# First modulation vectors in four column strips of TensorE, tokens loaded first, first dense products by halves of the features

## The chip, the cores and the metric

One NeuronCore of a Trainium2 chip runs the kernel. The metric is device time in microseconds for one execution. TensorE is called PE below, VectorE DVE, ScalarE ACT, GpSimd POOL, and SyncE, which issues nearly all transfers, SP.

## What is computed

Two layers of a backbone for 512 latent tokens (x) and 256 context tokens (c), 1024 features, all in float32. Cut to what matters here:

```python
for l in range(2):
    mx = split(silu(c) @ w_mod[l] + b_mod[l], 6)          # six vectors of 1024: shift, scale, gate, twice
    mc = split(silu(c_ctx) @ w_mod[l] + b_mod[l], 6)
    hc = rmsnorm(ctx, g_pre_mix[l]) * (1 + mc[1]) + mc[0]
    h  = rmsnorm(x,   g_pre_mix[l]) * (1 + mx[1]) + mx[0]
    p  = h @ w_in[l]          # decays, keys, queries, values, gates, convolution and spatial-gating inputs
    y  = mixers(p)            # short conv | bidirectional gated DeltaNet in chunks | spatial gating
    x  = x + mx[2] * rmsnorm(y @ w_o[l], g_post_mix[l])
    ...                       # then a SwiGLU feed-forward, modulated by mx[3], mx[4], mx[5]; the context likewise
```

So nothing dense can start before shift and scale of the first norm are there: columns 0 to 2047 of `w_mod[0]`, 8.4 MB, multiplied by two vectors of 1024.

## The kernel before

Products of float32 operands are made from high and low parts (`hh`, `hl` of the features, `wh`, `wl` of the weights): three one-pass matmuls in a rounded format per 128 rows of contraction. Only the modulation, transposes and a few small sums are plain float32 matmuls.

**Who sets the order.** `Builder` writes the program along an estimated timeline: each part of the work is a task that yields a time or a condition, and of the tasks that can go on the one with the lowest priority number does (`run_tasks`). PE keeps the order written. Tables of numbers (`K`) hold priorities, depths and the events that tasks wait for. Every transfer is issued on SP (`dma`, line 430).

**Opening.** `cond` makes `csilu`, the silu of the two conditioning vectors as 128 x 16. `mod_pe` (line 804) takes `w_mod` in tiles `mw` of 128 rows x 512 columns (256 KB). Eight of them, the contraction, make one block of 512 columns: `ps[:2, :] += csilu[:, k::8]^T mw`, two rows of a bank `ps`. The four blocks come in the order 2, 3 (scale), 0, 1 (shift); 6 tiles may be loaded ahead. `mod_columns` turns the two rows into columns by four small transposes (`modr`), adds the bias, and `mod_ready` derives the factors when both blocks of a part are there. `layer_vectors` loads the biases, gains and convolution taps as rows `vrows` by eight small transfers and transposes them once.

**Norms.** `start` loads a stream's tokens only when half of block 2 (context) or block 3 (x's event is `half0_1`) has been multiplied, then `pre_norm` (line 874) squares, waits for all of shift and scale, scales by the reciprocal root (`xn`), transposes 128 x 128 pieces into a bank and modulates each of 8 feature tiles: `hh` on ACT, `hu` = high part less shift on ACT, low part on DVE.

**First dense products.** `keys` (line 1052) takes the first three weights (16 columns of decays and rates, the keys and the queries of head 0) stream by stream: all of the context's, then all of x's, so that neither waits for the other.

```python
for s, cond in zip(sts, conds or ()):
    yield cond                                   # hc0, then hx0
    for i, job in enumerate(jobs[:staged]):      # staged = 3
        ...
        yield from self.accumulate(ps, ws[i], self.hl(s[1]), (0, s[0].T), width(job))
```

Behind them follow the decays (`gates`, their rows `rh`), the triangular systems, the inverse of the context's chunks (DVE, `ivt`, `ivv`, `ivb`), that of x's, the scans, the output projections (`yh`) and the feed-forward. Modulation blocks 4 and later come mostly elementwise on DVE (`macc`), some on PE. Buffers of up to 512 columns are handed out from 66 slots; smaller ones share a slot if one is half used.

## Time and profile before

| | |
|---|---|
| median of 3 runs | 1831.14 us (1827.82 to 1832.52) |
| span of the profiled execution | 1826.1 us; its page gives no other time of it |
| PE, DVE, ACT busy | 97%, 70%, 41% of the span |
| read from memory | 233 MB, 136 GB/s over the span |

The page is one execution by the hardware profiler, and its span runs from the first to the last instruction. A share of busy time is a mean over stages with different limits, and PE's busy time is modelled. The window view gives the same per stretch, the timeline the instructions one by one, the views of waits who released whom.

### The profile page before, as it was taken

The page shows a single profiled execution, that of the slowest core. Times are in us where ns is not written, and L with a number is a line of the kernel's source. Part 1 is how long each engine was busy: PE and PEld are TensorE (multiplying, and loading weights), DVE is VectorE, ACT ScalarE, POOL GpSimd, SP SyncE. Part 2 cuts the span into 40 slices and gives each one's busy share as a digit, 9 for nine tenths or more (in the row PEclk, how much of TensorE's full clock was granted, in tenths as well). Part 3 has the DMA queues.
Part 4 walks back from the last instruction along what each step waited for, and adds up shares of the span by engine and source line. Part 5 has one row for each costly group of instructions (what it writes and reads, how often), then busy time and mean ns, then how long its engine had stood idle before and what let it go on. Part 6 is the DMA issues. An engine that isn't in the chain of part 4 may idle for free.

```text
span 1826.1 us, 27432 instructions
## 1 busy us (share of the span) xinstructions
PE 1765.4 (97%) x10319; PEld 1495.7 (82%) x10319; DVE 1269.5 (70%) x2414; ACT 750.3 (41%) x1659; POOL 107.1 (6%) x267
## 2 busy tenths in 40 slices
PE   7899999979999999999999999999899999999998
PEld 2588788869799888888788899878789898888886
DVE  1899877958769877623679867679968884344446
ACT  3764446254474222111464435467343752212122
POOL 0011002101000000000002000003000100000000
PEclk9999999989999999999999999999999999999999
DMA  8742321235578755533352436433333763333334
GB/s 281 249 129 83 95 67 36 79 112 164 173 223 273 222 177 188 153 104 116 106 156 81 127 118 174 137 93 86 89 127 116 230 198 93 100 96 93 104 93 138
DMA packets 288869, 250.15 MB, mean 137 GB/s; under 512 B 14544, under 2 KB 219350, under 8 KB 288736
## 3 DMA queue, kind: packets, MB, share of 16 engines
q1 hardware_dynamic: 288736, 248.40, 44.9%
q8 instruction: 81, 1.33, 0.3%
q14 instruction: 52, 0.43, 0.1%
HBM read 233.28 MB, written 15.07 MB: 136 GB/s over the span
## 4 chain that ended last, share of the span: by engine, by line
PE 71%; DVE 14%; ACT 6%; DMA 4%; issue 3%; POOL 2%; SPq 1%; DVEq 0%; POOLq 0%; ACTq 0%
PE ps L453 69%; DVE wl_l L465 2%; DVE ivt_l L465 2%; PE ps L457 2%; ACT junk L509 2%; DVE ivv_l L465 2%; DMA mw_b<-in_w_mod_dram 1%; ACT wh_l L509 1%; DVE dt_b L465 1%; DVE ivb_l L481 1%; DVE iva_l L481 1%; ACT L509 1%; SPq L430 1%; ACT xn_b L509 1%; DVE macc_b L461 1%
## 5 line engine op out<-in xcount | busy, mean ns | idle before, releaser
L453 PE MATMUL ps<-hh_b,wh_l 128*128 128x256 f32 (+2 forms) x2640 | 726.9, 325 | 8.1 <-DVE hh_b L461 2.5
L453 PE MATMUL ps<-hh_b,wl_l 128*128 128x512 f32 (+2 forms) x2000 | 665.2, 333 | 1.5 <-DVE wl_l L465 1.5
L453 PEld LDWEIGHTS ps<-hh_b,wh_l 128*128 128x128 f32 (+1 forms) x2640 | 456.3, 189 | 61.1 <-issue 5.5
L453 PE MATMUL ps<-hl_b,wh_l 128*128 128x512 f32 (+2 forms) x1360 | 483.9, 356 | 0.0
L465 DVE TENSOR_TENSOR wl_l<-wf_l,wh_l 128x1024 fp32r<-128x1024 f32 (+1 forms) x301 | 362.3, 1206 | 151.3 <-ACT wh_l L509 143.4
L453 PEld LDWEIGHTS ps<-hh_b,wl_l 128*128 128x128 f32 (+1 forms) x2000 | 377.0, 188 | 40.0 <-DVE wl_l L465 2.1
L509 ACT ACTIVATE wh_l<-wf_l 128x1024 fp32r<-128x1024 f32 x197 | 205.0, 1042 | 374.4 <-DMA wf_l<-in_w_ffn_in_dram 119.0
L453 PEld LDWEIGHTS ps<-hl_b,wh_l 128*128 128x128 f32 (+1 forms) x1360 | 256.6, 189 | 33.7 <-issue 0.2
L453 PE MATMUL ps<-wh_l,ah_b 128*128 128x512 f32 x576 | 204.6, 390 | 0.0
L453 PE MATMUL ps<-wl_l,ah_b 128*128 128x512 f32 x440 | 171.6, 390 | 0.9 <-DVE wl_l L465 0.8
L473 DVE CAST wh_l<-wf_l 128x1024 fp32r<-128x1024 f32 (+1 forms) x104 | 71.5, 687 | 130.7 <-PE ps L453 47.3
L461 DVE SCALAR_TENSOR_TENSOR macc_b<-mw_b,csilu,macc_b 128x512 f32<-128x512 f32 x196 | 142.5, 747 | 19.7 <-DMA mw_b<-in_w_mod_dram 13.2
L453 PEld LDWEIGHTS ps<-wh_l,ah_b 128*128 128x128 f32 x576 | 108.1, 188 | 22.9 <-DVE ah_b L465 0.3
L453 PE MATMUL ps<-wh_l,al_b 128*128 128x512 f32 x304 | 118.4, 389 | 0.0
L453 PEld LDWEIGHTS ps<-wl_l,ah_b 128*128 128x128 f32 x440 | 82.6, 188 | 18.6 <-DVE wl_l L465 1.8
L509 ACT ACTIVATE at_b<-ps 128x512 f32<-128x512 f32 (+1 forms) x71 | 33.9, 480 | 127.1 <-PE ps L453 122.0
L509 ACT ACTIVATE ah_b<-at_b 128x512 fp32r<-128x512 f32 (+1 forms) x62 | 33.4, 538 | 108.7 <-DVE at_b L465 108.7
L453 PE MATMUL ps<-wh_l,yh_b 128*128 128x512 f32 x192 | 74.1, 404 | 0.1
L453 PEld LDWEIGHTS ps<-wh_l,al_b 128*128 128x128 f32 x304 | 57.1, 188 | 11.8
L465 DVE TENSOR_TENSOR ivt_l<-ivv_l,ivb_l 128x31 f32<-128x31 f32 (+15 forms) x124 | 60.1, 485 | 3.5
L453 PE MATMUL ps<-wl_l,yh_b 128*128 128x512 f32 x160 | 62.6, 391 | 0.0
L465 DVE TENSOR_TENSOR at_b<-ps,at_b 128x512 f32<-128x512 f32 (+1 forms) x71 | 38.8, 547 | 31.8 <-PE ps L453 31.8
(511 smaller groups left out, 2140.8 us busy)
## 6 DMA issues: line engine op xcount, KB each, us to landing
wf_l<-in_w_ffn_in_dram SPq DMA_DIRECT2D x132, 512.0 KB, 4.5
mw_b<-in_w_mod_dram SPq DMA_DIRECT2D x208, 256.0 KB, 4.3
wf_l<-in_w_ffn_out_dram SPq DMA_DIRECT2D x66, 512.0 KB, 3.8
wf_l<-in_w_in_dram SPq DMA_DIRECT2D x64, 512.0 KB, 4.1
wf_l<-in_w_o_dram SPq DMA_DIRECT2D x32, 512.0 KB, 3.7
us_b<-sd SPq DMA_DIRECT2D x26, 256.0 KB, 2.8
xd<-x_b SPq DMA_DIRECT2D x20, 256.0 KB, 4.6
x_b<-xd SPq DMA_DIRECT2D x20, 256.0 KB, 2.9
```

Source lines behind the costliest of these rows:

```text
L430: self.nc.sync.dma_start(out, in_)
L453: self.nc.tensor.matmul(out, lhsT, rhs, start=start, stop=stop)
L457: self.nc.tensor.transpose(out, in_, self.ident[:m, :m])
L461: self.nc.vector.scalar_tensor_tensor(out=out, in0=in0, scalar=scalar, in1=in1, op0=op0, op1=op1)
L465: self.nc.vector.tensor_tensor(out=out, in0=a, in1=b, op=op)
L473: self.nc.vector.tensor_copy(out, in_)
L481: self.nc.vector.transpose(out, in_)
L509: self.nc.scalar.activation(out=out, in_=in_, func=func, **kw)
```

## The change

- `mod_pe` multiplies tile k into strip `32 * (k % 4)` of the bank: 32 columns of the array, with a stationary operand of 32 columns (`cs4`: the two vectors and 30 zeros), so that four consecutive tiles use four strips. A sum over the strips (`sel4`) takes the place of the transposes. 16 tiles may be loaded ahead in place of 6. The blocks come in the order 2, 0, 3, 1, so scale and shift of the first 512 features are complete after two blocks.
- Tokens of both streams and the first two weights are loaded ahead of `w_mod`. The eight small transfers of `vrows` are issued on ACT.
- `pre_norm` with `halves` squares, scales and transposes without waiting, and modulates four features when their half of the factors is there; `mod_ready` derives factors by block.
- `keys` takes the three staged products by halves of the contraction (the context's queries alone stay whole), both streams in each half.
- `cs4` takes half of a slot and is never freed, so buffers of 256 columns use its other half one after another.

```diff
-     'mpe': 6,
+     'mpe': 16,
...
-    def dma(self, out, in_):
-        self.nc.sync.dma_start(out, in_)
+    def dma(self, out, in_, side=False):
+        (self.nc.scalar if side else self.nc.sync).dma_start(out, in_)
...
+        self.sel4 = self.cp.tile([P, 32], F32, name="sel4")
+        self.vtt(self.sel4, self.ident[:, 0:32], self.ident[:, 32:64], ALU.add)
+        for g in (2, 3):
+            self.vtt(self.sel4, self.sel4, self.ident[:, 32 * g:32 * g + 32], ALU.add)
...
-        ld = lambda r0, ap, n: self.dma(rows[r0:r0 + n, :], ap)
+        ld = lambda r0, ap, n: self.dma(rows[r0:r0 + n, :], ap, l == 0)
...
+        self.cs4 = self.blk("cs4", 32 * KD).ap.rearrange("p (k m) -> p k m", k=KD)
+        self.pset(self.cs4, 0.0)
+        self.vcopy(self.cs4[:, :, 0:2], s.rearrange("p (s k) -> p k s", k=KD))
...
-            yield from self.mod_columns(v, b, ps, (0, 1))
+            r = self.blk("modr")
+            self.act(r.ap, ps)
+            pc = yield from self.gtile(r.ap)
+            for i in range(4):
+                self.matmul(pc[:, 2 * i:2 * i + 2], r.ap[:, P * i:P * i + P], self.sel4[:, 0:2])
+            r.free()
+            self.mod_bias(v, b, pc, streams)
...
-            self.matmul(ps[:2, :], self.csilu[:, k::8], raw.ap, start=(k == 0), stop=(k == KD - 1))
+            g = 32 * (k % 4)
+            self.matmul(ps[g:g + 32, :], self.cs4[:, k, :], raw.ap, start=(k < 4), stop=(k >= 4), share=3)
...
-        yield self.modulated(v["l"], part, part + 1)
-        self.ev.add(name)
+        if not halves:
+            yield self.modulated(v["l"], part, part + 1)
+            self.ev.add(name)
...
+            if halves:
+                yield lambda: all(f"block{v['l']}_{2 * p + hf}" in self.ev for p in (part, part + 1))
+                self.ev.add(name if hf else name + "_half")
...
-        for s, cond in zip(sts, conds or ()):
-            yield cond
-            for i, job in enumerate(jobs[:staged]):
-                if len(ws) == i:
-                    ws.append((yield from feed.take()))
-                yield self.room(8)
-                ps = yield from self.bank()
-                yield from self.accumulate(ps, ws[i], self.hl(s[1]), (0, s[0].T), width(job))
...
+        for hf in range(2 if staged else 0):
+            for s, cond in zip(sts, conds[hf]):
+                yield cond
+                st = s[0]
+                for i, job in enumerate(jobs[:staged]):
+                    whole = st.T < SEQ and i == staged - 1
+                    if whole and not hf:
+                        continue
...
+                    yield from self.accumulate(ps, ws[i], self.hl(s[1]), (0, st.T), width(job),
+                                               range(KD) if whole else range(4 * hf, 4 * hf + 4))
...
-            yield on("half0_2" if st is sc else K["wx"])
             xs = self.load(st, src)
-            yield from self.pre_norm(st, xs, vs[0], 0, hs, name=name)
+            yield from self.pre_norm(st, xs, vs[0], 0, hs, name=name, halves=True)
...
-        spawn(0, self.mod_pe(0, vs[0], [2, 3, 0, 1], (0, 1), K["mpe"]))
-        spawn(0, start(sc, I["ctx"][0], cx, hc, "hc0"))
-        spawn(0, first_weights())
-        spawn(K["plv"], self.layer_vectors(0, vs[0]))
-        spawn(K["psx"], start(sx, I["x"][0], x, hx, "hx0"))
+        spawn(-1, self.layer_vectors(0, vs[0]))
+        spawn(0, start(sc, I["ctx"][0], hc, "hc0"))
+        spawn(0, start(sx, I["x"][0], hx, "hx0"))
+        spawn(0, self.mod_pe(0, vs[0], [2, 0, 3, 1], (0, 1), K["mpe"]))
+        f.add(self.keys_w(0, False) + self.cols_w(0, OFF_V, NH))
```

Line 453 of the kernel before (the matmul of the helper) is line 452 of the changed one. The order in which the program issues its work moves at three places that matter below.

**PE, first products of the modulation.** Before (`mw` are tiles of `w_mod`, `modr` the two rows of a finished block):

```order
L457 MATMUL ps_65<-ident,vrows_b_8_130 128x128
L453 MATMUL ps_64<-mw_b_9_141,csilu 2x512
L453 MATMUL ps_64<-mw_b_10_144,csilu 2x512
L453 MATMUL ps_66<-mw_b_11_147,csilu 2x512
L453 MATMUL ps_66<-mw_b_12_150,csilu 2x512
```

With the change (`cs_b_2_116` is the slot that `cs4` shares, first with `vrows`; `xn` are scaled tokens):

```order
L457 MATMUL ps_64<-ident,cs_b_2_116 128x128
L452 MATMUL ps_65<-mw_b_17_164,cs_b_2_116 32x512
...
L452 MATMUL ps_65<-mw_b_23_176,cs_b_2_116 32x512
L457 MATMUL ps_64<-ident,xn_b_63_257 128x128
L452 MATMUL ps_65<-mw_b_24_178,cs_b_2_116 32x512
L457 MATMUL ps_64<-ident,xn_b_64_259 128x128
L457 MATMUL ps_64<-ident,xn_b_65_261 128x128
L457 MATMUL ps_64<-ident,xn_b_66_263 128x128
L452 MATMUL ps_67<-sel_106,modr_b_75_289 128x2 x4
```

The first seven products stand behind the transpose of `vrows`, the eighth and all later ones behind the first transpose of x's scaled tokens (`xn_b_63`).

**ACT, ahead of those scaled tokens.** With the change:

```order
L509 ACTIVATE pick_122<-ones 128x1 x2
L428 DMA cs_b_2_116<-in_b_mod_dram 48x128
...
L428 DMA cs_b_2_116<-in_g_onorm_dram 1x128
L509 ACTIVATE xn_b_45_225<-x_b_5_138,rx_c 128x512
L509 ACTIVATE junk,sx_x<-x_b_9_147 128x512
...
L509 ACTIVATE junk,sx_x<-x_b_16_159 128x512
L509 ACTIVATE xn_b_63_257<-x_b_9_147,rx_x 128x512
```

Eight transfers are issued here and eight squares of x follow; before, ACT issued none, and x's squares stood behind block 1's rows.

**PE, end of the modulation.** With the change (`hh_b_40`, the context's fourth feature):

```order
L452 MATMUL ps_63<-hh_b_40_220,wh_l_35_205 128x256 x2
L452 MATMUL ps_63<-hh_b_40_220,wl_l_36_206 128x256
L452 MATMUL ps_69<-mw_b_81_314,cs_b_2_116 32x512
L452 MATMUL ps_69<-mw_b_82_317,cs_b_2_116 32x512
L452 MATMUL ps_69<-mw_b_83_320,cs_b_2_116 32x512
L452 MATMUL ps_65<-sel_106,modr_b_95_404 128x2 x4
L457 MATMUL ps_68<-ident,xn_b_85_352 128x128
```

The last three of the 32 products stand behind the dense products of the first four features of the context; before, all 32 stood ahead of every dense product.

## Rows read from the trace of the kernel before

**Rows 1.** The page, busy time of each engine.

```profile
PE 1765.4 (97%) x10319; PEld 1495.7 (82%) x10319; DVE 1269.5 (70%) x2414; ACT 750.3 (41%) x1659; POOL 107.1 (6%) x267
```

**Rows 2.** Windows of the opening: busy us per engine (instructions), granted clock, DMA share, GB/s.

```profile
25.00:30.00 5.00, 5.00 (x13) 1.02 (x12) 0.00 (x0) 1.52 (x3) 0.00 (x0) 1.00 1.05 388
...
40.00:45.00 5.00, 2.57 (x18) 1.41 (x16) 1.64 (x7) 5.00 (x16) 0.00 (x0) 1.00 0.67 213
...
45.00:50.00 5.00, 1.24 (x7) 0.69 (x7) 1.16 (x4) 4.04 (x10) 1.02 (x1) 0.72 0.71 221
...
50.00:55.00 5.00, 4.92 (x27) 4.56 (x28) 4.94 (x11) 5.00 (x11) 0.00 (x0) 0.60 1.05 349
```

**Rows 3.** Timeline of the opening: start us, us, engine, line, operation, tiles.

```profile
4.43 7.87 PE L453 MATMUL ps<-mw_b,csilu 128*2 128x512 f32 x12 [1.25 <-DMA mw_b<-in_w_mod_dram]
...
7.43 0.33 SPq L430 DMA_DIRECT2D vrows_b<-in_b_mod_dram  x1
...
12.21 0.22 SPq L430 DMA_DIRECT2D vrows_b<-in_g_onorm_dram  x1
...
19.56 0.63 ACT L509 ACTIVATE junk<-x_b 128x512 f32<-128x512 f32 x1
...
20.31 0.63 ACT L509 ACTIVATE junk<-x_b 128x512 f32<-128x512 f32 x1
...
20.86 17.33 PE L453 MATMUL ps<-mw_b,csilu 128*2 128x512 f32 x40 [1.18 <-DMA mw_b<-in_w_mod_dram]
...
38.22 0.59 ACT L509 ACTIVATE modr_b<-ps 2x512 f32<-2x512 f32 x1 [6.28 <-DMA x_b<-in_x_dram]
...
40.04 0.24 DVE L469 TENSOR_SCALAR neg_l<-mod_l 128x8 f32<-128x8 f32 x2
```

**Rows 4.** Timeline where the first dense products run.

```profile
48.01 0.16 DVE L461 SCALAR_TENSOR_TENSOR mx_x<-sx_x 128x4 f32<-128x4 f32 x1 [2.71 <-ACT junk L509]
...
49.31 0.72 ACT L509 ACTIVATE xn_b<-x_b,rx_x 128x512 f32<-128x512 f32 x1 [0.93 <-POOL rx_x L485]
...
50.08 0.69 PE L457 MATMUL ps<-ident,xn_b 128*128 128x128 f32 x2 [2.26 <-ACT xn_b L509]
...
50.86 1.02 ACT L509 ACTIVATE hh_b<-ps,mod_l 128x256 fp32r<-128x256 f32 x2
...
53.22 1.92 ACT L509 ACTIVATE hh_b<-ps,mod_l 128x512 fp32r<-128x512 f32 x3
...
60.96 2.73 DVE L461 SCALAR_TENSOR_TENSOR macc_b<-mw_b,csilu,macc_b 128x512 f32<-128x512 f32 x4
...
65.29 1.91 PE L457 MATMUL ps<-ident,xn_b 128*128 128x128 f32 x16
```

**Rows 5.** Timeline of PE where the third product of x ends.

```profile
92.22 0.39 PE L453 MATMUL ps<-hl_b,wh_l 128*128 128x512 f32 x1
...
92.45 0.40 PE L453 MATMUL ps<-hh_b,wl_l 128*128 128x512 f32 x1
```

**Rows 6.** Instructions on the decay rows rh_b and on ivb_l: form, count, ns, first and last start.

```profile
L453 PE MATMUL ps<-rh_b,sel x16: 378/386/500, 88.7 to 282.1; 40*128 40x256 f32 x8, 40*128 40x512 f32 x8
...
L481 DVE STREAM_TRANSPOSE ivb_l<-ivv_l x2: 2114/2124/2135, 213.8 to 362.5; 128x1024 f32<-128x1024 f32 x2
```

**Rows 7.** Window in which DVE works on the first inverse.

```profile
120.00:150.00 30.00, 30.00 (x183) 26.18 (x182) 29.29 (x77) 18.29 (x63) 6.71 (x18) 1.00 0.18 55
```

**Rows 8.** Waits of PE from 200 to 400 us: total, times, longest.

```profile
PE ps L453 <- ACT Q_b L509: 8.6, 1, 8.6
```

**Rows 9.** Instructions on hu_b, 900 to 1500 us, and the waits of PE in the norms there.

```profile
L509 ACT ACTIVATE hu_b<-hh_b,neg_l x30: 497/509/527, 905.4 to 1475.9; 128x256 f32<-128x256 f32 x30
...
L461 DVE SCALAR_TENSOR_TENSOR hl_b<-ps,mod_l,hu_b x22: 474/479/485, 1181.7 to 1476.4; 128x256 fp32r<-128x256 f32 x22
...
PE ps L457 <- ACT xn_b L509: 3.3, 3, 2.2
```

More of the change, by code (lines that the diff above doesn't have):

```diff
@@ L44 @@
      'pout1': 1,
-     'psx': 0,
-     'plv': 1,
      'pmx0': 0,
@@ L584, in dense, with accumulate @@
         return out
-    def accumulate(self, ps, w, xs, seg, M=P, order=None, o=0):
+    def accumulate(self, ps, w, xs, seg, M=P, ks=None):
         _, _, wh, wl = w
-        sl, xc = slice(*seg), slice(seg[0] - o, seg[1] - o)
+        sl = xc = slice(*seg)
         K = len(xs)
-        n = 0
-        for i, k in enumerate(order or range(K)):
+        ks = range(K) if ks is None else ks
+        n = 3 * ks[0]
+        for i, k in enumerate(ks):
             xh, xl = (a[:, xc] for a in xs[k])
@@ L790, in mod_ready @@
     def mod_ready(self, l, v, b, streams):
-        part = b // 2
-        self.ev.add(f"block{l}_{b}")
-        if f"block{l}_{b ^ 1}" not in self.ev:
-            return
-        for s in streams:
-            t = v["mod"][:, s, 8 * part:8 * part + 8]
-            if part in (1, 4):
-                self.stt(t, t, 1.0, v["cols"][:, R_GPM if part == 1 else R_GPF:][:, :8], ALU.add, ALU.mult)
-            if part in (0, 3):
-                self.vts(v["neg"][:, s, 8 * part:8 * part + 8], t, -1.0, None, op0=ALU.mult)
-        self.ev.add(f"mod{l}_{part}")
+        part, o = b // 2, 4 * (b % 2)
+        for s in streams:
+            t = v["mod"][:, s, 4 * b:4 * b + 4]
+            if part in (1, 4):
+                self.stt(t, t, 1.0, v["cols"][:, (R_GPM if part == 1 else R_GPF) + o:][:, :4], ALU.add, ALU.mult)
+            if part in (0, 3):
+                self.vts(v["neg"][:, s, 4 * b:4 * b + 4], t, -1.0, None, op0=ALU.mult)
+        self.ev.add(f"block{l}_{b}")
+        if f"block{l}_{b ^ 1}" in self.ev:
+            self.ev.add(f"mod{l}_{part}")
     def mod_pe(self, l, v, blocks, streams, ahead=3):
@@ L829, in mod_pe @@
                 self.spawn(0, columns(b, ps))
-            if k == 3:
-                self.ev.add(f"half{l}_{b}")
     def mod_v(self, l, v, blocks, streams):
@@ L872, in tiles, with pre_norm @@
         return range(seg[0] // P, seg[1] // P)
-    def pre_norm(self, st, x, v, part, hs, seg=None, name=""):
+    def pre_norm(self, st, x, v, part, hs, seg=None, name="", halves=False):
         seg = seg or (0, st.T)
         T, ts = seg[1] - seg[0], self.tiles(seg)
-        if not hs:
-            hs += [(self.blk("hh", st.T), self.blk("hl", st.T)) for _ in range(KD)]
         sl = slice(*seg)
@@ L886, in pre_norm @@
         r = self.rstd(st, ss, ts, "x")
-        yield self.modulated(v["l"], part, part + 1)
-        self.ev.add(name)
+        if not halves:
+            yield self.modulated(v["l"], part, part + 1)
+            self.ev.add(name)
+        if not hs:
+            hs += [(self.blk("hh", st.T), self.blk("hl", st.T)) for _ in range(KD)]
         per = 512 // T
@@ L1078, in keys @@
             use(job, sts[0], ps)
-        ws = []
-        for s, cond in zip(sts, conds or ()):
-            yield cond
-            for i, job in enumerate(jobs[:staged]):
-                if len(ws) == i:
-                    ws.append((yield from feed.take()))
-                yield self.room(8)
-                ps = yield from self.bank()
-                yield from self.accumulate(ps, ws[i], self.hl(s[1]), (0, s[0].T), width(job))
-                self.done.append(ps)
-                use(job, s, ps)
-                if s is sts[-1]:
-                    self.drop(ws[i][:2])
+        ws, pss = [], {}
+        for hf in range(2 if staged else 0):
[6 more added lines that the diff above has]
+                        continue
+                    if len(ws) == i:
+                        ws.append((yield from feed.take()))
+                    if whole or not hf:
+                        yield self.room(8)
+                        pss[st, i] = yield from self.bank(3 if whole else 2)
+                    ps = pss[st, i]
+                    yield from self.accumulate(ps, ws[i], self.hl(s[1]), (0, st.T), width(job),
+                                               range(KD) if whole else range(4 * hf, 4 * hf + 4))
+                    if hf:
+                        self.done.append(ps)
+                        use(job, s, ps)
+                        if s is sts[-1]:
+                            self.drop(ws[i][:2])
         for job in jobs[max(len(first), staged):]:
@@ L1898, in fill1 @@
             self.drop(hx1)
-        def first_weights():
-            yield on("half0_0")
-            f.add(self.keys_w(0, False) + self.cols_w(0, OFF_V, NH))
         def dense():
@@ L1908, in dense @@
             spawn(K["pm0"], chain(self.wait(K["wm0b"]), self.later_mods(v)))
-            yield from self.keys(f, sts, v, False, staged=K["staged"], conds=[on("hc0"), on("hx0")])
+            yield from self.keys(f, sts, v, False, staged=K["staged"],
+                                 conds=[[on("hc0_half"), on("hx0_half")], [on("hc0"), on("hx0")]])
             yield from self.gdn_v(f, sts, v)
```

13 lines of the change are left out of this document (8 added, 5 removed).

## The prediction

> **What bounds the kernel now.** I read the page first: PE is busy 97% of the span, DVE 70%, ACT 41% [rows 1], so over the whole kernel there is almost nothing to gain except PE's work itself and the places where it lacks some. Those I looked for with the windows: in 40 to 45 us PE is busy 2.57 us of 5, in 45 to 50 only 1.24, and the granted clock is 0.72 there and 0.60 (of 2.4 GHz) in the next five [rows 2]. The timeline tells why. The 32 modulation products stand in it as two records each, 40 records in 17.33 us [rows 3], so 0.433 us a record and 0.87 a product: 27.7 us of PE by themselves, from 4.43 to about 38.2, with holes early on, where SP issues the eight small `vrows` transfers at (12.21 - 7.43) / 7 = 0.68 us each [rows 3]. The last product's rows are read at 38.22, the factors are derived at 40.28: 2.1 us for that chain. x's tokens come only now: its squares end at 48.01, its scaled tokens start at 49.31, PE's steady work at 50.08 [rows 4]. From there PE is held by little: one wait of 8.6 us behind x's inverse [rows 8], a few us in each norm [rows 9]. So the opening, some 45 us in which PE does no dense work, is where the change acts.
>
> **Pitches I use.** A one-pass product of 512 columns 0.23 us (92.22 to 92.45) [rows 5], of 256 half of it, 0.12; a transpose 1.91 / 16 = 0.12; ACT per feature 1.02 / 2 = 0.51 for 256 columns and 1.92 / 3 = 0.64 for 512; `macc` 2.73 / 4 = 0.68 [rows 4]; a square 20.31 - 19.56 = 0.75 [rows 3].
>
> **The opening with the change, step by step.**
>
> Data. Tokens and two weights are 3.73 MB and the first 16 tiles 4.19 MB. The first product starts at 4.43 [rows 3] with 0.26 MB there, so data starts near 3.7. At 350 GB/s (between 349 and 388, [rows 2]) the 7.92 MB are there at 26.3, the other 16 tiles at 388 GB/s at 37.1.
>
> ACT. By the order, x's first transpose stands ahead of all products but seven, behind the eight issues and eight squares on ACT. The context's 1.05 MB are there at about 6.7, its four squares (4 x 0.75) end near 10. The price of an issue on ACT isn't in the trace: between nothing and SP's 0.68 [rows 3], so 0 to 5.4 us; I take the middle, 2.7, for lack of a nearer row. Then the scaling of a context tile 0.72 and eight squares 6.0: 19.4. From the squares' sum to the scaled tokens 1.3 (48.01 to 49.31), the scaling 0.72 [rows 4]: 21.5, between 18.8 and 24.2.
>
> Strips. Two consecutive products in different strips may run side by side; the trace has none. Bounds: 0.87 (no overlap, [rows 3]) and a quarter of it, 0.22. Since the two records of one product can't overlap I take half, 0.43. The nine products left at 21.5 take 3.9, twelve transposes 1.4, the reading of them 0.4: block 0 ends at 27.2, after its data. With 2.1 for the factors, the first half can be modulated at 29.3.
>
> What a page has on this: "TensorE: Matmul & The Clock Gate", section "Measured speedup vs the span model", of the Trainium skill gives 2.38x for three column strips. No run here shows it; by its figure a product would cost 0.87 / 2.38 = 0.37 and the opening 1 us less.
>
> First halves. Four features of each stream on ACT: 8 x 0.51 + 7 x 0.64 = 8.5, so 37.8; the block-1 products left behind the context's fourth feature are three, with PE's part of that feature: 12 x 0.12 + 3 x 0.43 = 2.7, so 40.5; their data came at 37.1, so ACT ends last here. The second half of the factors is there at 42.6, and from there PE should be steady.
>
> To the same place. I compare at the end of x's third staged product, 92.7 before [rows 5]. With the change, by the order, 48 products of 256 (5.8), 60 of 512 (13.8), 36 transposes (4.3) and small ones (2) stand between: 25.9, so 68.5. That is 24.2 us earlier. But eight products of later modulation blocks (0.87 each) stood ahead of that place before and stand behind it now, since both programs have 16 of them: 6.9 us that return. **Net 17.3.**
>
> **What gives back.**
>
> *The inverses.* Behind the dense fill, PE waits for DVE's inverses, and DVE is busy 29.29 of 30 us in 120 to 150 [rows 7]. Decay rows are first multiplied at 88.7 [rows 6]; with the change about 21 earlier. But by the order ten more `macc` (0.68) and two more roundings of weights (1.1 each) stand between the first decays and the context's inverse (the whole program has as many as before): 9 us. The chain is then 12 us earlier where PE is 17. Of the missing 5, the order covers up to 5.5 with 24 output-projection products that moved ahead of the first use of the inverse. Bounds 0 to 5, I take 1 (PE now waits 8.6 once, [rows 8]).
>
> *The shared half slot.* All 256-column `hu` now take one buffer in turn: 0.51 on ACT, then 0.48 on DVE, one after the other [rows 9], where ACT alone needs 2 x 0.51 a feature. Nearly hidden; for 52 uses at 0 to 0.08 each, 0 to 4 us. I take 1.
>
> *Sixteen later products in strips*, in runs of up to six: from -5.2 (0.52 saved in ten of them) to +2.6 (0.16 lost at each end, below). I take -1.
>
> Sum: 1826.1 - 17.3 + 1 + 1 - 1 = 1809.8 of span. The shown median, 1831.14, lies 5.0 above the profiled span, and I add that: **1815**, 0.9% faster. A measurement of this kernel can tell about 0.3% (5.5 us) from no change.
>
> **Rivals.**
>
> R1, *strips don't overlap* (what the change says it does, it doesn't): 0.87 a product. For: the trace has no two products side by side. Against: nothing in it excludes it. 3.9 more for the nine, 1.3 for the last three, -1 becomes 0: about **1821**. Chance 0.11.
>
> R2, *each change between strips and whole array costs PE its fill.* A one-pass product of 512 is recorded with 0.39 us and followed after 0.23 [rows 5]: up to 0.16 us of overlap is lost at such a change. Some 15 groups of strips in the opening and 8 later, two changes each: 46 x 0.16 = 7.4 us, **1822**. A rule speaks for it: "Changing tiling mode (not just tile) drains the TensorE" ("TensorEngine Tiling (Array Packing)", section "Key Properties", the Trainium skill). No run here shows it; the opening has slack around ACT, which is against the full price. Chance 0.10.
>
> R3, slower: *DVE's chain doesn't come earlier with PE.* DVE is full from 120 on [rows 7]; the change brings elementwise work that PE's early start pulls ahead of the inverse (9 us). If first decays come no earlier than 88.7 - 9 = 80 the inverse is late by what they slip, PE's fill is used up 17 us sooner, and the wait at x's inverse (8.6, [rows 8]) grows to some 35. That is 9 beyond before: **1840**. For: ACT does more ahead of the decays; against: my forecast has them at 67, 13 us short of the point. Chance 0.11.
>
> R4, *all of it comes back*: the fill is just used up at x's inverse, where PE waits already; the chain there starts earlier only by what the 9 us leave and the covering products don't help: **1829**. Chance 0.12.
>
> **How the numbers follow.** Forecast 0.56; R1, R2 and the forecast are faster: 0.77. R4 is within 0.3% (1825.6 to 1836.6): 0.12; R3 slower: 0.11. Low end: strips at their best (-4), an issue on ACT free (-2.7), inverses and slot free (-2), and 3 for the unknown rate of data: 1803. High end: R1, R2 and R4 inside, 1831; R3 is left out, and a little below the low end.
>
> **What would show it.** Each product in strips should start 0.43 us after its neighbour (0.87: R1; a gap of 0.1 to 0.2 at the first whole-array product behind: R2). Factors of the first half near 29 us, of the second near 43, PE steady from there, the end of x's third product near 68, the first use of decay rows near 67, the wait at x's inverse at most 10. If steady work begins after 50, or that wait is over 20 us, the forecast is wrong, and by R3 rather than by the opening if the third product ends before 75. ACT's eight issues should lie between 0 and 0.68 us each.

## The result, and the profile after

The changed kernel takes **1859.4 us** (median of 4 runs, 1854.2 to 1861.1) where the kernel before took 1829.5 beside it: a ratio of **1.0157, 95% interval 1.0141 to 1.0173**, 1.6% slower. The forecast was 1815 with a range to 1831, so it has the wrong sign. The profiled span went from 1826.1 to 1859.4 us, 33.3 more.

PE's busy time on the page is the same as before to 0.1 us [rows 1], so its idle time has grown by the 33 us. (Time lost to a low clock counts as busy, and what the strips save on PE hides it in this sum.)

```profile
PE 1765.5 (95%) x10343; PEld 1501.5 (81%) x10343; DVE 1276.4 (69%) x2444; ACT 747.3 (40%) x1648; POOL 110.0 (6%) x268
```

To find where, I made one calculation on every trace. Each matmul record gets the same price in every run (0.21 us per 512 columns, at least 0.06; 0.43 per record of a `w_mod` product), and the prices are summed in order of start. The table says how much later than the kernel before (minus: earlier) a run has done the work that before had done at the time at the head of the column. From 480 on an entry is good to about 2 us: with other prices, the mean time from start to start of each form of matmul over all runs, none moves by more. Ahead of that the kinds of work in the two orders differ more, and with those prices the first row has -5.5 at 62 and 1.2 at 424, and single entries there move by 6 and 9. The other runs are those of the experiments.

| us later than before, at | 62 | 225 | 424 | 480 | 502 | 550 | 1446 | 1505 |
|---|---|---|---|---|---|---|---|---|
| the change | -1.4 | -5.9 | -3.0 | 18.5 | 23.9 | 24.6 | 25.3 | 31.8 |
| e1_six_ahead | 1.3 | -3.3 | 3.7 | 6.9 | 8.8 | 6.5 | 14.7 | 18.8 |
| e2_pace | -1.7 | -5.1 | 4.1 | 6.9 | 8.0 | 9.1 | 9.3 | 15.5 |
| e3_before_pace | 0.9 | 2.1 | 5.4 | 4.4 | 4.3 | 2.1 | 13.3 | 15.3 |
| e4_no_strips | 3.0 | 6.4 | 16.1 | 15.4 | 14.9 | 15.2 | 16.7 | 17.3 |
| e5_out_early | -1.4 | -5.9 | -2.0 | 5.7 | 7.3 | 11.8 | 15.2 | 21.1 |
| e6_mods_held | -1.5 | 6.4 | 8.7 | 6.6 | 7.7 | 6.1 | 10.4 | 18.3 |
| e7_no_halves | -1.2 | -6.3 | 0.1 | -0.6 | 0.5 | -1.5 | 7.2 | 13.2 |
| e8_true_costs | 2.7 | -3.5 | 7.4 | 9.2 | 10.2 | 10.8 | 23.3 | 25.5 |
| e9_slot_back | -1.1 | -5.7 | -1.8 | 20.1 | 23.8 | 24.1 | 29.3 | 31.7 |
| e10_no_halves_slot_back | -3.6 | -8.6 | -1.7 | -2.2 | -1.2 | -3.4 | 6.5 | 6.7 |
| e11_no_halves_slot_back_pace | -2.6 | -7.6 | -1.8 | -1.9 | -0.9 | -3.1 | 8.4 | 10.8 |
| e12_tiles_first | 0.7 | -6.9 | -1.8 | 0.9 | 2.6 | 0.9 | 17.5 | 19.3 |
| e13_tiles_first_no_halves | 0.5 | -4.8 | 0.0 | -0.3 | 0.8 | 0.6 | 13.6 | 16.2 |

For the change the first row reads: 6 us gained up to 225, lost again by 455, about 23 us lost between 455 and 502 at the end of x's mixers in layer 1, little from there to 1446, then 6.5 in layer 2's last norm.

Most of the 6 us are not the opening's. The same calculation puts the change 0.4 us ahead at 100, 0.7 at 150 and 5.4 at 200. Between 150 and 200 PE is busy throughout in both kernels, and there stand 15 of the sixteen later products that now run in strips. Windows of the instructions on `mw_b` alone, the first 32 products and the sixteen later ones with the change, then the sixteen before:

```profile
16.00:52.00 36.00, 20.94 (x64) 3.23 (x64) 0.00 (x0) 0.00 (x0) 1.00 0.95 319
52.00:620.00 568.00, 9.25 (x32) 1.37 (x32) 67.90 (x94) 7.12 (x10) 0.96 0.43 134
```

```profile
52.00:620.00 568.00, 15.20 (x32) 2.02 (x32) 73.80 (x103) 6.68 (x10) 0.99 0.47 143
```

The sixteen take 6.0 us less of PE.

**The opening.** The four windows of [rows 2], and one more:

```profile
25.00:30.00 5.00, 4.79 (x26) 2.35 (x25) 0.40 (x3) 0.85 (x2) 0.00 (x0) 1.00 1.05 395
40.00:45.00 5.00, 5.00 (x20) 1.22 (x19) 2.05 (x4) 3.48 (x7) 0.00 (x0) 1.00 0.84 211
45.00:50.00 5.00, 5.00 (x25) 2.15 (x26) 0.00 (x0) 0.00 (x0) 0.00 (x0) 1.00 0.73 229
50.00:55.00 5.00, 4.75 (x40) 3.67 (x34) 2.14 (x9) 2.11 (x5) 0.00 (x0) 1.00 0.91 295
55.00:60.00 5.00, 2.72 (x20) 1.99 (x20) 3.02 (x5) 4.97 (x8) 0.00 (x0) 1.00 1.07 365
```

The hole of before at 40 to 50 us is gone and the clock stays at its upper level: PE is busy. But it is busy with slow work: about half of 40 to 50 goes to `w_mod` products and the rest mostly to products with 16 columns. The timeline shows them (start, duration, engine, line, operation; what answers to [rows 3] and [rows 5]):

```profile
4.80 8.04 SPq L428 DMA_DIRECT2D x_b<-in_x_dram  x8
...
11.01 0.56 ACTq L428 DMA_DIRECT2D cs_b<-in_g_pre_mix_dram  x1
...
14.02 0.27 ACTq L428 DMA_DIRECT2D cs_b<-in_g_onorm_dram  x1
14.06 20.61 SPq L428 DMA_DIRECT2D mw_b<-in_w_mod_dram  x32
...
17.32 3.84 PE L452 MATMUL ps<-mw_b,cs_b 128*32 128x512 f32 x6 [0.82 <-DMA mw_b<-in_w_mod_dram]
...
22.29 0.72 ACT L509 ACTIVATE xn_b<-x_b,rx_x 128x512 f32<-128x512 f32 x1 [1.32 <-POOL rx_x L485]
...
30.00 1.90 PE L452 MATMUL ps<-mw_b,cs_b 128*32 128x512 f32 x10
...
33.89 0.24 DVE L469 TENSOR_SCALAR neg_l<-mod_l 128x4 f32<-128x4 f32 x2
...
43.83 1.04 PE L452 MATMUL ps<-mw_b,cs_b 128*32 128x512 f32 x2
44.80 0.40 PE L452 MATMUL ps<-hh_b,wl_l 128*16 128x512 f32 x1
...
49.65 1.06 PE L452 MATMUL ps<-mw_b,cs_b 128*32 128x512 f32 x6
50.64 1.05 PE L452 MATMUL ps<-sel,modr_b 128*128 128x2 f32 x8
...
53.43 0.24 DVE L469 TENSOR_SCALAR neg_l<-mod_l 128x4 f32<-128x4 f32 x2
...
83.14 0.39 PE L452 MATMUL ps<-hh_b,wl_l 128*128 128x512 f32 x1
```

A product alone between others, in the kernel before:

```profile
72.21 1.02 PE L453 MATMUL ps<-mw_b,csilu 128*2 128x512 f32 x2
73.16 0.40 PE L453 MATMUL ps<-hh_b,wh_l 128*16 128x512 f32 x1
```

A product is two records. Five in a row (x10) take 1.90 us, three (x6) 50.64 - 49.65 = 0.99, but a single one takes 44.80 - 43.83 = 0.97. A whole-array product in the same position took 73.16 - 72.21 = 0.95 before (0.87 in a run). The strips do run side by side; the ones that stand alone between other products gain nothing, and of the last ten products five stand alone. So all 32 last from 17.3 to 50.6, 33.3 us, against 33.8 before (4.43 to about 38.2, [rows 3]). Factors of the first half come at 33.9, of the second at 53.4. x's third product ends near 83.5, 9.2 earlier than [rows 5]; less the 6.9 us of products that merely moved behind it, that is some 2 us (0.4 by the table's calculation at 100).

**The chain to the inverses.** On the decay rows `rh_b`, on `dt_b` in the second direction and on the inverse `ivb_l` in layer 1, to be read beside [rows 6]. The times of a row are the first and the last start, for `ivb_l` those of the context and of x:

```profile
L452 PE MATMUL ps<-rh_b,sel x16: 381/436/497, 81.8 to 297.3; 40*128 40x256 f32 x8, 40*128 40x512 f32 x8
...
L461 DVE SCALAR_TENSOR_TENSOR dt_b<-ps,gc_c,mm_b x8: 340/344/351, 100.6 to 112.0; 128x128 f32<-128x128 f32 x8
...
L481 DVE STREAM_TRANSPOSE ivb_l<-iva_l x2: 2070/2072/2075, 183.9 to 340.3; 128x1024 f32<-128x1024 f32 x2
L481 DVE STREAM_TRANSPOSE ivb_l<-ivv_l x2: 1896/1989/2082, 225.8 to 376.1; 128x1024 f32<-128x1024 f32 x2
```

Before, the second and third were:

```profile
L461 DVE SCALAR_TENSOR_TENSOR dt_b<-ps,gc_c,mm_b x8: 340/342/351, 101.2 to 112.3; 128x128 f32<-128x128 f32 x8
...
L481 DVE STREAM_TRANSPOSE ivb_l<-iva_l x2: 2059/2075/2091, 167.9 to 323.3; 128x1024 f32<-128x1024 f32 x2
```

Decay rows are used 6.9 us earlier (81.8 for 88.7), but the first transpose of the context's inverse starts 16.0 later (183.9 for 167.9) and its last 12.0 later (225.8 for 213.8 [rows 6]); x's last starts at 376.1 for 362.5. Below, an inverse ends or comes at the start of its last transpose.

What PE waited for in the whole run (total, times, longest), against the one wait of [rows 8]:

```profile
PE ps L457 <- ACT xn_b L509: 29.3, 9, 12.1
PE ps L452 <- ACT yh_b L509: 9.2, 2, 8.7
PE ps L452 <- ACT U_b L509: 6.8, 1, 6.8
```

For `xn_b` it waited 13.4 us before. The wait for `U_b` ends at 228.3, and ACT copies `U_b` from the context's inverse: this is the late chain's direct price, 6.8 us. Between 200 and 300 the kernel before has no wait over 0.4 us. The wait for `yh_b` stands near x's inverse, where that for `Q_b` stood, and is as long (8.7 for 8.6).

**The hole at 470 to 487.** Windows of the kernel before, then of the changed one:

```profile
455.00:470.00 15.00, 15.00 (x77) 12.57 (x76) 13.51 (x20) 7.76 (x13) 3.44 (x2) 1.00 0.60 175
470.00:485.00 15.00, 13.57 (x66) 10.83 (x65) 13.08 (x20) 9.46 (x21) 2.28 (x1) 1.00 0.71 230
485.00:505.00 20.00, 20.00 (x93) 16.62 (x92) 10.84 (x17) 7.13 (x17) 0.00 (x0) 1.00 0.36 104
```

```profile
455.00:470.00 15.00, 12.02 (x76) 10.27 (x76) 10.90 (x25) 9.07 (x33) 5.47 (x5) 1.00 0.95 323
470.00:485.00 15.00, 4.68 (x16) 2.73 (x15) 11.91 (x19) 9.49 (x20) 5.86 (x2) 0.50 0.81 279
485.00:505.00 20.00, 18.57 (x105) 15.98 (x103) 16.50 (x28) 11.32 (x21) 0.00 (x0) 0.95 0.34 108
```

PE is busy 35.3 us of 50 where it was 48.6: 13.3 less; and the 4.7 us of work in 470 to 485 and some 2 behind it ran at the lower clock (0.50 granted), which is another 3.4. Together 16.7 in these 50 us. PE's timeline shows what stood there:

```profile
469.37 0.66 PE L457 MATMUL ps<-ident,o_b 128*128 128x128 f32 x4 [2.22 <-DVE o_b L465]
469.78 2.24 PE L452 MATMUL ps<-wh_l,yh_b 128*128 128x512 f32 x4
476.17 1.12 PE L457 MATMUL ps<-ident,wsr_b 128*128 128x128 f32 x4 [4.14 <-DVE us_b L461]
483.43 2.15 PE L457 MATMUL ps<-ident,xn_b 128*128 128x128 f32 x8 [6.14 <-ACT xn_b L509]
...
485.80 0.63 PE L452 MATMUL ps<-wh_l,yl_b 128*128 128x512 f32 x1
```

Four products of the output projection (`yh_b`), then two things that are not ready: transposes of `wsr_b` that wait for DVE's `us_b`, and the context's next norm (`xn_b`). PE keeps the order written. Before, some 70 products of the output projection stood between the last transposes of `o_b` and that norm; now they stand behind it.

**Layer 2's last norm.** The 15 pieces on the shared half slot (`cs_b`) there, and before them the same 15 of the kernel before, on `hu_b`:

```profile
L509 ACT ACTIVATE hu_b<-hh_b,neg_l x15: 497/509/521, 1442.0 to 1475.9; 128x256 f32<-128x256 f32 x15
...
L509 ACT ACTIVATE cs_b<-hh_b,neg_l x15: 492/501/511, 1468.6 to 1517.3; 128x256 f32<-128x256 f32 x15
```

The same instructions of the same length (0.50 us) are spread over 48.7 us in place of 33.9. ACT stands in the timeline behind DVE, as the forecast had it, but PE then waits for both: 3.0 us for `hh_b` and `hl_b` from 1420 to 1540, where before it waited for `xn_b` alone [rows 9]. The longest of these waits stands in the second row:

```profile
1483.36 0.51 ACT L509 ACTIVATE cs_b<-hh_b,neg_l 128x256 f32<-128x256 f32 x1 [0.55 <-DVE hl_b L461]
...
PE ps L452 <- ACT hh_b L509: 1.4, 1, 1.4
```

### The profile page after: what moved, and what is told of

It reads as the page before. It is cut to its first block, busy times and chain, and to the rows that moved or that the text cites. A ratio compares the mean times of both kernels' runs of the same rounds, so it can differ in the third digit from the quotient of the medians.

```text
span 1859.4 us, 27458 instructions
## 1 busy us (share of the span) xinstructions
PE 1765.5 (95%) x10343; PEld 1501.5 (81%) x10343; DVE 1276.4 (69%) x2444; ACT 747.3 (40%) x1648; POOL 110.0 (6%) x268
## 5 line engine op out<-in xcount | busy, mean ns | idle before, releaser
L452 PE MATMUL ps<-hh_b,wl_l 128*128 128x512 f32 (+3 forms) x2000 | 665.6, 334 | 4.9 <-DVE wl_l L465 4.9
L509 ACT ACTIVATE wh_l<-wf_l 128x1024 fp32r<-128x1024 f32 (+1 forms) x187 | 194.2, 1040 | 314.3 <-DMA wf_l<-in_w_ffn_in_dram 121.3
L473 DVE CAST wh_l<-wf_l 128x1024 fp32r<-128x1024 f32 x114 | 78.2, 686 | 119.4 <-DMA wf_l<-in_w_ffn_in_dram 52.4
L452 PEld LDWEIGHTS ps<-wh_l,ah_b 128*128 128x128 f32 x576 | 108.1, 188 | 22.7 <-issue 0.3
L509 ACT ACTIVATE at_b<-ps 128x512 f32<-128x512 f32 (+1 forms) x48 | 25.5, 532 | 117.1 <-PE ps L452 117.1
L509 ACT ACTIVATE ah_b<-at_b 128x512 fp32r<-128x512 f32 (+1 forms) x42 | 25.4, 604 | 89.4 <-DVE at_b L465 89.4
L457 PE MATMUL ps<-ident,xn_b 128*128 128x128 f32 x176 | 28.8, 303 | 30.8 <-ACT xn_b L509 29.3
```

Source lines behind the costliest of these rows:

```text
L452: self.nc.tensor.matmul(out, lhsT, rhs, start=start, stop=stop)
L457: self.nc.tensor.transpose(out, in_, self.ident[:m, :m])
L473: self.nc.vector.tensor_copy(out, in_)
L509: self.nc.scalar.activation(out=out, in_=in_, func=func, **kw)
```

## The experiments

Two kinds of cause stood against each other. One is physical: the opening gains little, DVE's chain to the inverses is late, the slot serializes. The other is the order: the builder writes a program along its own estimates, the numbers in `K` fit the timeline of before, and any other opening redraws the order of everything behind it. All medians stand beside runs of the kernel before on the same chip (1831.3 to 1831.7).

### Two numbers that only move the order, and the same on the kernel before

e1_six_ahead: the changed kernel with

```diff
-     'mpe': 16,
+     'mpe': 6,
```

> The changed kernel with one number undone: 6 tiles of w_mod loaded ahead in place of 16; strips, tokens first and halves stay. Theory A (the order written behind the opening makes the loss; any small number redraws it): the opening stays as in the changed kernel (first use of the decay rows within 3 us of 81.8, first decays on DVE near 100.6), but the PE gaps between 375 and 565 us, 30 us now, fall below 12, and the time comes to 1825 to 1845 us. Theory B (the chain through DVE is late because of what the changed opening itself costs): same opening, same loss, 1853 to 1865 us.

Measured: 1849.9 us, ratio 1.0114 (1.0090 to 1.0138): between the two ranges expected.

e2_pace: the changed kernel, and e3_before_pace: the kernel before, each with the builder's lead

```diff
-K = {'ahead': 2.0,
+K = {'ahead': 2.1,
```

> The changed kernel with the builder's number 'ahead' at 2.1 in place of 2.0: it only says how far elementwise work is written ahead of its engine, so the same operations are issued in another order. Theory A: the time moves by 10 us or more from 1859 (to 1830 to 1848, or above 1870) with the opening as before it (decay rows first used at 80 to 84). Theory B: within 5 us of 1859.

> The kernel before with 'ahead' at 2.1 in place of 2.0, nothing else. Theory A: it loses too, 5 to 20 us (1835 to 1850), with the opening unchanged up to the decays at 88.7, because the numbers of the kernel before fit its own timeline and no other. Theory B: within 4 us of 1829.5, since DVE's chain starts and works as before.

Measured: the changed kernel 1846.0 us, 1.0087 (1.0062 to 1.0112), 13 less than without the edit; the kernel before 1842.5, 1.0063 (1.0048 to 1.0078), 11 more than without it. The edit takes nothing away and adds nothing. Up to 225 us e2 stands as the change does (-5.1 for -5.9), and the window at the place of the hole, 470 to 485, is full:

```profile
455.00:470.00 15.00, 12.27 (x67) 10.29 (x67) 12.35 (x24) 8.83 (x29) 3.78 (x3) 1.00 0.68 237
470.00:485.00 15.00, 14.86 (x70) 12.30 (x71) 14.41 (x23) 9.97 (x21) 1.61 (x1) 1.00 0.65 217
```

So the hole is no property of the new opening: it is where the order of this one program happened to fall. e1 has none either. Both still stand 8 to 9 us behind at 502, with x's inverse ending near 374 (362.5 before): that loss the edits leave. And the kernel before loses 11 us by the same kind of edit: the order alone is worth more than the opening's gain, in both directions.

### The strips

e4_no_strips: the changed kernel with the modulation multiplied as before (cut):

```diff
-            self.matmul(ps[g:g + 32, :], self.cs4[:, k, :], raw.ap, start=(k < 4), stop=(k >= 4), share=3)
+            self.matmul(ps[:2, :], self.csilu[:, k::8], raw.ap, start=(k == 0), stop=(k == KD - 1))
...
-            self.mod_bias(v, b, pc, streams)
+            yield from self.mod_columns(v, b, ps, (0, 1))
```

> The changed kernel without strips: tile products of two columns one after another (0.87 us each) and the small transposes, as before; tokens first and halves stay. If the strips carried a gain in the opening, the first use of the decay rows comes later than 81.8 by 32 x (0.87 - 0.45) = 13 us at most; if the opening is bound by the loads, by less than 5. Theory A: the total has little to do with that, anywhere from 1835 to 1870. Theory B: 1859 plus what the opening loses, 1862 to 1875.

Measured: 1847.7 us, 1.0094 (1.0077 to 1.0111). In its timeline the 32 products are one run of 64 records in 29.77 us, with nothing between them, and decay rows come 2.1 us later than with strips:

```profile
18.13 29.77 PE L452 MATMUL ps<-mw_b,csilu 128*2 128x512 f32 x64 [0.41 <-ACT cols_l L509]
...
L452 PE MATMUL ps<-rh_b,sel x16: 379/388/500, 83.9 to 269.4; 40*128 40x256 f32 x8, 40*128 40x512 f32 x8
```

By the table it is 4.4 us behind the change at 62 (and 3.6 by the same calculation at 100): that is what the strips are worth here. (Its last product ends at 47.9, earlier than the 50.6 with strips, since nothing else stands between.) In the total it is 12 us better than the change: its order has no hole at 470 (15.4 behind at 480, 14.9 at 502), though it has lost 16 by 424. The strips help where they act, and the total doesn't follow.

### Taking away the hole, and the chain's load

e5_out_early: x's output projection of layer 1 is made known to the builder with the end of the scans, as in layer 2, in place of behind the context's gated residual:

```diff
-            if l:
-                spawn(K["pout1"], out_x(l, segs, after))
+            spawn(K["pout1"] if l else K["pout0"], out_x(l, segs, after))
...
-            if not l:
-                spawn(K["pout0"], out_x(l))
```

> The changed kernel with x's output projection started as a task when the inverse is done in place of when its gated outputs are (as layer 2 has it). Up to 390 us the instructions and their order are those of the changed kernel. Theory A (what it loses between 424 and 505 us, 27 us, is the order of the output projections and the context's norms there): that loss falls by 12 us or more, the PE gaps at 469 to 484 go, and the time comes to 1838 to 1847 us. Theory B (DVE's chain, 12 to 17 us late from the first inverse on, sets the end of the stage): the chain is as late, so the time stays at 1853 to 1865.

Measured: 1851.5 us, 1.0119 (1.0099 to 1.0139). Up to about 390 us it is the program of the change, and x's inverse ends as late (376.9). PE's work between 455 and 505:

```profile
455.00:470.00 15.00, 12.71 (x77) 11.20 (x77) 9.02 (x25) 6.08 (x26) 3.03 (x3) 0.89 0.72 227
470.00:485.00 15.00, 14.44 (x80) 11.93 (x79) 10.27 (x18) 7.71 (x19) 1.43 (x2) 1.00 0.87 263
485.00:505.00 20.00, 19.41 (x95) 15.63 (x94) 18.88 (x32) 15.16 (x36) 2.38 (x2) 1.00 0.45 148
```

At 502 it is 7.3 behind where the change is 23.9. This splits the loss up to there: **16.6 us are the order at the end of x's mixers** (over the same work, 13.1 of them are idle time of PE and 3.4 its lower clock), and 7 remain. I put these down to the late chain, but that is argued: they arise between 455 and 470, behind both inverses, and at 424 the table has e5 not behind. About half of the 16.6 is lost again later (a wait of 6.4 us for `xn_b` near 541 is one place), so the total gains 7.9 and lies between the two ranges expected.

e6_mods_held: the next modulation's elementwise work on DVE is held back until the context's scan is gated, which takes 26 `macc` away from 60 to 168 us:

```diff
-     'wm0b': 'hx0',
+     'wm0b': 'gated_c0_0',
```

> The changed kernel with the four later modulation blocks (scale and shift of the feed-forward) held until the context's scan is gated: 32 macc in place of 60 stand on DVE ahead of the context's inverse. Theory B (DVE's work ahead of the first inverse makes the chain late): the context's inverse starts 15 us or more before 184, x's inverse ends at 360 or before in place of 376, and the time falls by 12 us or more, to 1847 or less. Theory A: the inverses come earlier all the same, but the 28 macc return behind them and the order is another draw: between 1845 and 1875 with no relation to the chain.

Measured: 1847.9 us, 1.0092 (1.0077 to 1.0107). The inverses move as a chain bound by DVE should:

```profile
L481 DVE STREAM_TRANSPOSE ivb_l<-iva_l x2: 2074/2075/2076, 142.3 to 318.5; 128x1024 f32<-128x1024 f32 x2
L481 DVE STREAM_TRANSPOSE ivb_l<-ivv_l x2: 1883/1993/2103, 190.4 to 353.4; 128x1024 f32<-128x1024 f32 x2
```

The context's inverse starts 41.6 us earlier than with the change, x's ends at 353.4, 22.7 earlier. Yet PE still waits, 10.3 us once between 200 and 400 (for `z_b`, in place of `yh_b`), and the run is 14.5 behind at 357. So DVE's load does set when the inverses come, and an earlier inverse by itself doesn't give the time back: at 480 e6 is 6.6 behind, much as e1 and e2. The total falls by 11.5 (12 or more was expected if the chain were the cause), and the hole at 470 is gone here too.

### The halves

e7_no_halves: the staged products wait for all eight features, as before:

```diff
-                                 conds=[[on("hc0_half"), on("hx0_half")], [on("hc0"), on("hx0")]])
+                                 conds=[[on("hc0"), on("hx0")], [on("hc0"), on("hx0")]])
```

> The changed kernel, but dense products wait for all of shift and scale, as before: strips, tokens first and modulation by halves stay. If the failed step of the opening is that the last products of w_mod stand one by one between dense ones (0.97 us each instead of 0.25), then without halves the strips run in fours, the second half of the factors is there near 43 in place of 53 us, and the decays come within 3 us of 81.8 or before. If halves carry a gain, the decay rows come 4 us or more later than 81.8. Total: theory A another draw, 1835 to 1860; theory B 1859 plus the shift of the decays.

Measured: 1841.7 us, 1.0058 (1.0043 to 1.0073). Up to 225 us it is no worse than the change (-1.2 and -6.3 for -1.4 and -5.9), with the second factors at 52.9 and the decay rows at 81.7: **the halves of the products carry nothing.** The expectation had the second factors near 43 if products that stand alone between dense ones were what held them back. That is a miss: no dense product stands between them here. PE waits instead for DVE's features ahead of x's next transposes, and the last products stand one or two at a time between such transposes:

```profile
40.52 0.66 PE L457 MATMUL ps<-ident,xn_b 128*128 128x128 f32 x4 [2.31 <-DVE hl_b L461]
```

x's inverse comes at 363.5, almost as before, and the run stands level with before to 550. This supports the 7 us of the chain: three runs with x's inverse 11 to 14 us late and no hole (e1, e2, e5) stand 5.7 to 6.9 behind at 480, this one level. It doesn't settle them: e12 has that inverse 6.5 us late and is 0.9 behind, e4 has it on time (362.5) and is 15.4 behind, e6 has it 9 us early and is 6.6 behind. e7 then loses 8.7 us between 550 and 1446, where the change loses 0.7.

### What the builder believes

e8_true_costs: the builder is told the measured prices: 0.97 us for the first of up to four strips in a row and 0.01 for the others, 0.4 for an issue on ACT; with a lead of 2.5.

```diff
-        self.spend("t", max(self.size(lhsT), self.size(rhs)) * (0.4262 if rhs.dtype == F32R else 1.7) / share, [out],
-                   [lhsT, rhs])
+        if share > 1:
+            n = 0.97 if self.strips % 4 == 0 else 0.01
+            self.strips += 1
...
+        self.spend("t", n, [out], [lhsT, rhs])
```

> The changed kernel whose builder is told what the trace shows of strips (0.97 us for the first of up to four in a row, 0.01 for the others, in place of a third of a product each) and of an issue on ACT (0.4 us), and 'ahead' 2.5; the operations are the same. Theory A: an order made for its own timeline gets most of the 28 us back, 1828 to 1842. Theory B: 1850 to 1865, since the chain through DVE is the same.

Measured: 1856.9 us, 1.0146 (1.0123 to 1.0169). Hardly better than the change. It lies in the range of the second theory. With these prices and this lead the order is no better, so the strips' wrong price alone does not explain it; the hole at 470 is gone (10.2 behind at 502), and 12.5 us are lost between 550 and 1446 instead.

### The shared half slot

e9_slot_back: `cs4` gives its half slot back where layer 2's dense products begin, after its last use:

```diff
-        self.cs4 = self.blk("cs4", 32 * KD).ap.rearrange("p (k m) -> p k m", k=KD)
+        self.cs4b = self.blk("cs4", 32 * KD)
+        self.cs4 = self.cs4b.ap.rearrange("p (k m) -> p k m", k=KD)
...
             hs = self.hl(hx1)
+            self.cs4b.free()
```

e10_no_halves_slot_back is that with e7's edit, and e11_no_halves_slot_back_pace is e10 with a lead of 2.1.

> The changed kernel that gives the slot of cs4 back when layer 2's dense products start, so that buffers of 256 columns take slots of their own again in layer 2; the program up to there is the same. Theory C (the half slot that all 256-column buffers take in turn is what every run with strips loses in layer 2's norm before the last feed-forward, 6 us where runs without strips lose under 1): that loss goes and the time falls by 4 to 9 us, to 1850 to 1855. Theory A alone (that loss too is just the order): within 3 us of 1859, or any other draw with the loss of 6 us in that norm still there.

> Dense products wait for all of shift and scale, and the slot of cs4 is given back at layer 2; strips and tokens first stay. Theory C: 6 us less than 1841.7 without the slot, 1833 to 1838. Theory A: layer 2 is drawn anew, 1836 to 1850.

> As the run before, with 'ahead' at 2.1. Theory A: the opening is the same within 3 us and the time is another draw, 5 us or more away from the run before; if the draw is a good one, 1826 to 1831, which would beat the kernel before by no more than the 2 to 6 us that the opening gives. Theory C says nothing of it.

Measured: e9 1863.0 us, 1.0168 (1.0155 to 1.0182); e10 1839.2, 1.0043 (1.0027 to 1.0058); e11 1839.7, 1.0037 (1.0023 to 1.0051). In e10 the 15 pieces take the time that they took before (33.8 us):

```profile
L509 ACT ACTIVATE hu_b<-hh_b,neg_l x15: 498/510/524, 1450.3 to 1484.1; 128x256 f32<-128x256 f32 x15
```

Between 1446 and 1505 the seven runs that hold the slot to the end (the change, e1, e2, e5 to e8) lose 2.2 to 7.9 us, 5.5 on the mean; the seven that don't (e3, e4, e9 to e13) 0.2 to 2.6, 1.7 on the mean. So the slot costs **about 4 us**; e9, the same program up to layer 2, loses 4.1 less there than the change (2.4 for 6.5). e9's total doesn't show it (1850 to 1855 was expected): it is 4.0 worse already at 1446, where its order in layer 2 is another. e11 misses its expectation of 5 us or more: a lead of 2.1 moves e10 by 0.5 us, where it moved the change by 13 and the kernel before by 11. e10 is the best of all versions of the change, and it is ahead of the kernel before up to 550 us; what it loses, it loses behind that.

### Tiles before tokens

e12_tiles_first: the slot given back, the modulation's task started ahead of x's, and 8 tiles ahead. e13_tiles_first_no_halves: the same order of tasks with 16 ahead, a lead of 2.1 and e7's edit.

```diff
-        spawn(0, start(sx, I["x"][0], hx, "hx0"))
         spawn(0, self.mod_pe(0, vs[0], [2, 0, 3, 1], (0, 1), K["mpe"]))
+        spawn(0, start(sx, I["x"][0], hx, "hx0"))
```

> The changed kernel with x's tokens loaded behind the first 8 tiles of w_mod (8 ahead in place of 16), and the slot of cs4 given back at layer 2; halves, strips and the context's tokens first stay. If the opening's gain was lost to the start of w_mod (first product at 17.3 us, 4.4 before, behind 3.7 MB of tokens and weights), the first product comes at 9 to 11, the factors of the first half at 28 or before (34.0 in the changed kernel), and the decay rows are first used at 76 or before (81.8). If ACT's squares of x or the products one by one are what holds, the first half comes early but the decays stay within 3 us of 81.8. Total by theory A: another draw; with the hole at 470 drawn away, 1828 to 1845.

> As the run before, without halves in the dense products, 16 tiles ahead and 'ahead' 2.1. If the start of w_mod is the opening's loss, all factors are there at 46 or before (53.0 without halves and tokens first) and the total falls below the 1839 of the same kernel with tokens first, to 1826 to 1836; if not, 1836 to 1845.

Measured: e12 1846.5 us, 1.0075 (1.0060 to 1.0091); e13 1846.0, 1.0087 (1.0071 to 1.0103). The first product starts at 11.3 and 11.5 in place of 17.3, but the second half of the factors comes at 55.5 and 54.6 (53.4), and decays at 81.5 and 83.4 (81.8). The first halves came at 35.7, where 28 or before was expected, and 27.0 (33.9). The late start of the modulation behind x's tokens was not what held the second half.

No version ran faster than the kernel before; the best are 0.4% slower.

## Why the prediction was wrong

**The opening: right in direction, 17.3 forecast, about 2 at the same place.** The failed step is "First halves": block-1 products done near 40.5 and the second half of the factors at 42.6. They came at 50.6 and 53.4. Of these 10 us, 4.6 were there with the first half of the factors (33.9, forecast 29.3), and ACT's features end as much later, near 42.4. The other 5.5 lie behind them. I had ACT as what ends last, with three products and 12 dense matmuls left for PE, 2.7 us; but PE had eight products (4.9 us) and 22 dense matmuls left, 8.5 us from 42.16 to 50.64, and was busy 10 us of 10 between 40 and 50. The price is part of it: 0.43 us a product holds for products in runs, one that stands alone between others takes 0.97, and I priced all by a mean although the order showed which stand alone. The eight would have taken 3.4 by it; all 32 are recorded with 20.9 us, 0.65 each. As to the first half, `w_mod` begins to be issued at 14.06, since x's eight transfers take 8.04 us of SP's queue, one us each. In e12 and e13 the products begin 6 us earlier, and the second half comes no earlier even so. Scaled tokens at 22.3 (forecast 21.5) and eight issues on ACT at 0.27 to 0.56 us (middle taken: 0.34) were right.

**"From there PE should be steady"** failed likewise: in 55 to 60 us PE is busy 2.72 of 5, while ACT is full (4.97 of 5) with features, a rounding of weights, a table load of 1.28 us and `wst`; PE waits 0.8 us for a feature and 1.3 for `wst`.

**The sixteen later products: a gain of 1 us taken, 6.0 measured** (9.25 for 15.20), beyond the low end of my bounds. Runs of three cost what one costs. This, and not the opening, is most of what the change has gained at 225.

**The inverses: taken as 1 us, they cost the wait of 6.8 for `U_b`, which uses up what was gained, and perhaps the 7 that are left in e5.** I had the chain 12 us earlier; it came 12 later. The added load was seen (10 `macc` and two roundings of weights forecast; 8 `macc` and 4 `al_b` came, 8.6 us of DVE, and one `wl_l` fewer). The earlier start was not there: the context's decays in the first direction begin on DVE at 87.7 (93.3 before), those in the second at 100.6 (101.2 before). From there to the inverse it took 83.3 us, before 66.7: 9.8 more of DVE's busy time and 6.8 more of its idle time, 3.6 of it one wait for a modulation block that PE multiplies. And the cover failed: the "24 output-projection products that moved ahead of the first use of the inverse" waited themselves for `yh_b`, 8.7 us, at the place where before Q_b was waited for [rows 8]. A product is cover only if its own operands are there.

**The order at the end of x's chain, 16.6 us, had no term at all.** I read the order around the opening and up to x's inverse, and not behind it, where the same table of numbers decides.

**The shared slot: 1 taken, about 4 measured**, the upper end of its bounds. I had reckoned the wait of ACT for DVE and left out PE, which waits in its turn.

The terms nearly add up: 7 put down to the chain, 16.6 for the order and 6.5 in the last norm are 30 of the 33.3; the 6 us gained up to 225 are used up by the wait of 6.8 for `U_b` right behind it. The 7 are argued from runs that differ in their order too; they were not isolated.

**The rivals.** R1 (no overlap) is false. R2 is false in size: a lone strip product takes 0.97 to the next start where a lone whole-array one took 0.95, and the pause ahead of it is the same (45.04 to 45.36, and 71.88 to 72.21 before). So some 0.02 is left for the change between strips and whole array, where I had 0.16 at each of its two sides. "TensorE: Matmul & The Clock Gate", "Measured speedup vs the span model", in the Trainium skill, gives 2.38x for three strips. The trace has somewhat more: three took 0.99 us here where three whole products take 3 x 0.87 = 2.61, so 2.6x. R3 came nearest: its turning point was "first decays no earlier than 80", and they came at 81.8. But it put its price of 9 at x's inverse, where the wait stayed 8.7 and did not grow to 35; the new wait, 6.8, stands at the context's. By the prediction's own sign the opening failed as well: the third product ended at 83.5, not before 75. R3 was given 0.11 because the forecast of the decays (67) was thought good to 13 us. R4, that all of the gain comes back, is what became of the gain up to 225. But R4's 1829 is 30 short of the result and R3's 1840 is 19 short, because none of my cases had the order lose anything by itself.

## What to carry to other kernels

Where a program's order comes out of a list scheduler with tuned numbers, test how much one number that only reorders is worth (here 11 us on the kernel before, 13 on the change, 0.5 on e10) ahead of believing in any smaller gain; the range must be at least that wide. Price work on an in-order engine by the instructions that stand beside it: strips are worth their factor only next to other strips. And for each piece of work counted as cover, look whether its own operands are there in time.

## What the runs showed of the hardware

A single float32 product in a strip of 32 columns took 0.97 us, two in different strips 0.98 (42.16 to 43.14), three 0.99 and five 1.90; over the whole array one took 0.87 in a run and 0.95 alone. I had not expected that strips would overlap so well in runs, or that a lone one would gain nothing. SP issued x's tokens at 1.0 us per 256 KB, but the 32 `w_mod` tiles of the same size at 0.64 (20.61 / 32), before at 13.36 / 20 = 0.67: a transfer's place on the queue isn't a fixed price. The clock granted to PE was 0.50, the lower of its two levels (1.2 GHz), from 470 to about 487, with waits of 2.2, 4.1 and 6.1 us that ended at 469, 476 and 483; a product of 512 columns was recorded with 0.63 us there (485.80) and with 0.39 behind it.
